# Three pads that move the weights' tiles against the moving operands of the matmuls

## The chip, the cores and the metric

One core of a Trainium2 chip runs the whole program once. The metric is the device time of one execution in microseconds (us). The engines are named as in the profile: PE is TensorE's matmul, PEld its weight load, DVE is VectorE, ACT ScalarE, POOL GpSimd, SP the queue that issues most DMAs. SBUF addresses below are bytes within a partition, and all of them follow from the order and the sizes in which the program allocates its tiles.

## The reference

Two blocks of two layers each over 256 tokens of width 2048, all in float32:

```
for l in range(2):                       # first block
    h = rms_norm(x, norm_w[l]);  p = h @ w_in[l]          # 2048 x 6668
    y = concat(window attention, conformer convolution, gated delta rule)   # all from p
    x = x + y @ w_out[l]                                   # 2048 x 2048
for l in range(2):                       # second block
    h = rmsnorm(x, ln1_g[l]);  proj = h @ w_in[l]          # 2048 x 6176
    x = x + concat(differential attention, GLA, retention) @ w_o[l]
    h = rmsnorm(x, ln2_g[l])
    u = conv3(h @ w_up[l]);  a, g = split(u)               # 2048 x 11264
    x = x + (a * silu(g)) @ w_down[l]                      # 5632 x 2048
return rmsnorm(x, final_g)
```

## The kernel before

All large products are made by one helper, `proj_t_unit` (lines 356 to 386). The residual x lies transposed in SBUF: features in the partitions, the 256 tokens along the row, four tiles of 512 features. Float32 precision is had by splitting both factors into a rounded part and a remainder (`split`, lines 249 and 250, and `norm_h`, lines 287 and 290): the normed residual becomes the tiles `hh` and `hl`, the weights become `wh` and `wl`. For each block of 128 x 128 weights, `product` issues three matmuls of 256 columns: wh with hh (L372), wh with hl (L373), wl with hh (L374). The weights are the stationary operand, loaded by PEld for each matmul (512 bytes of each partition), and the activations are the moving one (1024 bytes of each partition).

`wunit` brings the weights in units of 512 x 512: a DMA into `wr`, then ACT rounds into `wh` and DVE subtracts into `wl`, each with four buffers of 4096 bytes. The order of the instructions on each engine is made by the tile scheduler from the order of the program and its priorities.

Stages in order of time: `block1` twice (projections, attention, convolution, delta rule, then `add_x` with w_out), then `block2`, `ffn`, `block2`, `ffn`. In the blocks the matmuls of attention and delta rule are mixed into the stream by `pump`. In `ffn` the stream has nothing but `proj_t_unit`: eleven blocks of 512 columns of a and of g with the moving operand `hh`/`hl`, in two groups (six and five), and after each group the down projection with the activations `ah`/`al` as the moving operand. In a layer that is 1408 products with the normed residual and 704 with the activations, of three matmuls each.

What moves in `add_x` of the blocks are the tiles `yh`/`yl` (`put_y`). In `block1` the units 0 and 1 lie in the pool `hp`, where `hh` and `hl` also live, unit 2 has the tag "b4" and unit 3 the tag "z4". In `block2` the units 0 and 2 lie in `hp`, units 1 and 3 have the tag "p4".

**Addresses.** The pools are allocated one behind the other: `cp` (constants, with a first tile "pad0"), `hp` from 20160, `wp` behind it, `sp`, then the pool of the stage. Every buffer of `hh`, `hl`, `wr`, `wh`, `wl` is 4096 bytes, so all buffers of `hp` lie at 192 modulo 512, and all of `wh` and `wl` at 256 modulo 512, since "pad1" at the head of `wp` takes 64 bytes. The rows of a tile that one matmul or load reads start at multiples of 512 bytes in it. So one number, the start of the weights less the start of the moving operand modulo 512, tells how the two reads stand to each other; it is called the offset here. By the allocation it is, in the kernel before: 64 for `hh`/`hl`, for `yh`/`yl` in `hp`, and for `ah`/`al` in both FFN layers; 448 for `yh`/`yl` of tag "b4"; 160 for tag "z4"; 192 for tag "p4". In `proj_unit` (the untransposed projections, L424 to L426) the roles are changed: slices of `hh`/`hl` are stationary and 512 columns of the weights move.

Of the kernel before, what the change touches and what calls it, by code (L numbers as in the profile page):

```python
# [10 lines left out]
F32 = mybir.dt.float32  # L11
# [8 lines left out]
P = 128  # L20
# [113 lines left out]
class _Kernel:  # L134
    def __init__(self, ctx, tc, A):
        self.ctx, self.tc, self.nc, self.A = ctx, tc, tc.nc, A
        self.bg, self.ph, self.final = [], None, False
        self.cp = ctx.enter_context(tc.tile_pool(name="cp", bufs=1))
        self.cp.tile([P, 8], F32, name="pad0")
        self.hp = ctx.enter_context(tc.tile_pool(name="hp", bufs=4))  # L140
        self.wp = ctx.enter_context(tc.tile_pool(name="wp", bufs=3))
        self.wp.tile([P, 16], F32, name="pad1", bufs=1)
        self.sp = ctx.enter_context(tc.tile_pool(name="sp", bufs=2))
        self.pm = ctx.enter_context(tc.tile_pool(name="pm", bufs=2, space=PSUM))
        self.ps = ctx.enter_context(tc.tile_pool(name="ps", bufs=4, space=PSUM))
        self.dp = ctx.enter_context(tc.tile_pool(name="dp", bufs=1, space=DRAM))
        nc = self.nc
        self.base = self.cp.tile([P, 3 * P], F32, name="base")
        self.ident, self.le, self.gt = (self.base[:, i * P:(i + 1) * P] for i in range(3))
        self.ones = self.cp.tile([P, P], F32, name="ones")  # L150
        nc.vector.memset(self.ones, 1.0)
        self.lmask = self.cp.tile([P, 7, P], mybir.dt.uint8, name="lmask")
        self.xd = [A["xt"][g] for g in range(4)]
        self.gws = self.cp.tile([P, 112], F32, name="gws")
        self.fg = self.gws[:, 96:112]
        self.early = None
# [858 lines left out]
    def attention(self):  # L1015
# [9 lines left out]
        for t in range(2):  # L1025
            yield
            nc.vector.tensor_mul(qk[t], qk[t], r[:, t].unsqueeze(2).broadcast_to([P, 16, 64]))
            for i, (h0, h1) in enumerate(((0, 12), (12, 16))):
                n = h1 - h0
                xr = qk[t][:, h0:h1, 0:16]  # L1030
                a = self.sml([P, 12, 16], "ra", 2)
                b = self.sml([P, 12, 16], "rb", 2)
                bro = lambda v: v.unsqueeze(1).broadcast_to([P, n, v.shape[-1]])
                nc.vector.tensor_mul(a[:, :n], xr, bro(tb[:, t, i, 0]))
                nc.vector.tensor_mul(b[:, :n, 0:8], xr[:, :, 8:16], bro(tb[:, t, i, 1, 0:8]))
                nc.vector.tensor_mul(b[:, :n, 8:16], xr[:, :, 0:8], bro(tb[:, t, i, 1, 8:16]))
                nc.vector.tensor_add(xr, a[:, :n], b[:, :n])
            nc.gpsimd.tensor_copy(kd[t], qk[t][:, 12:16].unsqueeze(2).broadcast_to([P, 4, 2, 64]))
# [414 lines left out]

    def ffn(self, l, follow):
        nc, A = self.nc, self.A
        fc = self.param(A["fc2"][l], "fc2")
        cw = [fc[:, 2 * NF * i:2 * NF * (i + 1)] for i in range(3)]
        cb = fc[:, 6 * NF:]
        for b0, b1 in ((0, 6), (6, 11)):
            act = []  # L1460
            for b in range(b0, b1):
                cv = []
                for s in range(2):
                    ps = self.proj_t(A["w_up_2"][l], [(s * FF + b * 512, 512)])
                    u = self.tt("u", [P, 4, T], "u")
                    with self.tc.high_priority():
                        nc.vector.tensor_mul(u, ps, self.bcn(4))
                    c = self.ph.tile([P, 4, T], F32, tag=f"c{s}", name=f"c{s}", bufs=2)
                    col = lambda t, q: t[:, s * NF + b * 4 + q:s * NF + b * 4 + q + 1]
                    for q in range(4):  # L1470
                        nc.scalar.activation(c[:, q], u[:, q], AF.Identity, bias=col(cb, q), scale=col(cw[1], q))
                    for q in range(4):
                        nc.vector.scalar_tensor_tensor(c[:, q, 1:], u[:, q, :T - 1], col(cw[0], q), c[:, q, 1:],
                                                       op0=ALU.mult, op1=ALU.add)
                    for q in range(4):
                        nc.vector.scalar_tensor_tensor(c[:, q, :T - 1], u[:, q, 1:], col(cw[2], q), c[:, q, :T - 1],
                                                       op0=ALU.mult, op1=ALU.add)
                    cv.append(c)
                nc.scalar.activation(cv[1], cv[1], AF.Silu)
                nc.vector.tensor_mul(cv[0], cv[0], cv[1])  # L1480
                ah = self.ph.tile([P, 4, T], F32R, tag="ah", name="ah", bufs=7)
                al = self.ph.tile([P, 4, T], F32R, tag="al", name="al", bufs=7)
                self.split(cv[0], ah, al)
                act.append((ah, al, b * 512))
            self.add_x(A["w_down_2"][l], act, follow=follow if b1 == 11 else None)
# [121 lines left out]
```

## Time and profile before

| | |
|---|---|
| three runs | 3399.01, 3340.39 and 3395.86 us, median 3395.86 us |
| the profiled execution | 3369.48 us, of which the span from the first to the last instruction is 3367.7 us |
| PE busy | 3308.9 us (98%), 26498 matmuls |
| DVE, ACT, POOL busy | 2175.3 us (65%), 1636.5 us (49%), 259.8 us (8%) |
| mean granted TensorE clock | 0.988 |
| DMA | 602.64 MB, 179 GB/s over the span |

The busy time of PE is the union of matmuls that overlap (a matmul's record is about 280 ns long while the next one starts some 115 ns after it), so a busy share near 100% says that PE never waits, not how fast it goes. How fast it goes is read from the starts: the time from one matmul's start to the next, by the timeline or by the number of matmuls in a window.

### The profile page before, as it was taken

How to read it: one execution, taken by the hardware profiler on the slowest of the kernel's cores; microseconds unless marked ns; L12 is line 12 of the kernel's file. 1: busy time of each engine (PE TensorE's matmuls, PEld its weight loads, DVE VectorE, ACT ScalarE, POOL GpSimd, SP SyncE). 2: the span in 40 equal slices, each digit the busy share in tenths (PEclk: the TensorE clock that was granted, in tenths of full speed). 3: DMA queues.
4: the chain of work that ended last, by engine and by line, in shares of the span. 5: the costliest groups of instructions: out<-in, count | busy, mean ns of one | idle time of the engine just before them, and what ended most of it. 6: DMA issues, size and time to landing. Idle time of an engine off the chain costs nothing. (4 is left out here: it accounts for less than half of the span.)

```text
span 3367.7 us, 63948 instructions
## 1 busy us (share of the span) xinstructions
PE 3308.9 (98%) x26498; PEld 3191.5 (95%) x26498; DVE 2175.3 (65%) x3183; ACT 1636.5 (49%) x2202; POOL 259.8 (8%) x477
## 2 busy tenths in 40 slices
PE   8999989999999999999999999999999999999998
PEld 8899989899998988999999999999899999999998
DVE  8887558886565557666654776555665666546664
ACT  5555444554455444455543554554454455435453
POOL 1210010210010010100000000200101000000000
PEclk9999989999999999999999999999999999999999
DMA  7554476553566555566656665655545555555554
GB/s 221 153 166 135 163 205 191 150 172 112 177 218 208 160 163 154 187 190 198 195 193 194 193 194 195 212 155 159 171 148 188 189 186 185 188 188 185 187 186 144
DMA packets 351652, 602.64 MB, mean 179 GB/s; under 512 B 35314, under 2 KB 92154, under 8 KB 351360
## 3 DMA queue, kind: packets, MB, share of 16 engines
q1 hardware_dynamic: 346800, 585.15, 55.7%
q0 software_dynamic: 4560, 13.40, 1.4%
q8 instruction: 207, 3.39, 0.4%
q14 instruction: 85, 0.70, 0.1%
HBM read 589.40 MB, written 11.15 MB: 178 GB/s over the span
## 5 line engine op out<-in xcount | busy, mean ns | idle before, releaser
L250 DVE TENSOR_TENSOR wl<-wr,wh 128x1024 fp32r<-128x1024 f32 (+2 forms) x1094 | 1308.0, 1198 | 880.7 <-ACT wh L249 878.0
L249 ACT ACTIVATE wh<-wr 128x1024 fp32r<-128x1024 f32 (+2 forms) x1096 | 1128.8, 1032 | 1436.0 <-PE pt L373 1131.4
L372 PE MATMUL pt<-hh,wh 128*128 128x256 f32 x5184 | 1457.8, 281 | 8.3 <-ACT wh L249 8.3
L374 PE MATMUL pt<-hh,wl 128*128 128x256 f32 x5184 | 1457.8, 281 | 3.6 <-DVE wl L250 3.6
L373 PE MATMUL pt<-hl,wh 128*128 128x256 f32 x5184 | 1453.0, 280 | 0.0
L372 PEld LDWEIGHTS pt<-hh,wh 128*128 128x128 f32 x5184 | 985.3, 190 | 21.2 <-ACT wh L249 9.6
L374 PEld LDWEIGHTS pt<-hh,wl 128*128 128x128 f32 x5184 | 979.4, 189 | 9.0 <-DVE wl L250 4.4
L373 PEld LDWEIGHTS pt<-hl,wh 128*128 128x128 f32 x5184 | 980.8, 189 | 4.5 <-issue 4.1
L372 PE MATMUL pt<-ah,wh 128*128 128x256 f32 x1328 | 369.6, 278 | 0.0
L373 PE MATMUL pt<-al,wh 128*128 128x256 f32 x1328 | 369.6, 278 | 0.0
L374 PE MATMUL pt<-ah,wl 128*128 128x256 f32 x1328 | 369.6, 278 | 0.0
L372 PE MATMUL pt<-yh,wh 128*128 128x256 f32 x1024 | 292.4, 286 | 12.4 <-ACT wh L249 7.7
L373 PE MATMUL pt<-yl,wh 128*128 128x256 f32 x1024 | 292.3, 285 | 2.0 <-DVE yl L250 2.0
L374 PE MATMUL pt<-yh,wl 128*128 128x256 f32 x1024 | 291.3, 285 | 1.2 <-DVE wl L250 1.2
L372 PEld LDWEIGHTS pt<-ah,wh 128*128 128x128 f32 x1328 | 251.9, 190 | 0.0
L373 PEld LDWEIGHTS pt<-al,wh 128*128 128x128 f32 x1328 | 249.2, 188 | 0.0
L374 PEld LDWEIGHTS pt<-ah,wl 128*128 128x128 f32 x1328 | 249.2, 188 | 0.0
L372 PEld LDWEIGHTS pt<-yh,wh 128*128 128x128 f32 x1024 | 198.3, 194 | 13.6 <-ACT wh L249 8.4
L373 PEld LDWEIGHTS pt<-yl,wh 128*128 128x128 f32 x1024 | 198.3, 194 | 3.3 <-DVE yl L250 3.3
L374 PEld LDWEIGHTS pt<-yh,wl 128*128 128x128 f32 x1024 | 199.0, 194 | 1.7 <-DVE wl L250 1.7
L425 PE MATMUL pn<-wl,hh 128*128 128x512 f32 (+1 forms) x448 | 170.1, 380 | 0.8 <-DVE wl L250 0.7
L426 PE MATMUL pn<-wh,hl 128*128 128x512 f32 (+1 forms) x448 | 169.4, 378 | 0.0
(585 smaller groups left out, 3091.5 us busy)
## 6 DMA issues: line engine op xcount, KB each, us to landing
wr<-in_w_up_dram SPq DMA_DIRECT2D x352, 512.0 KB, 4.0
wr<-in_w_in_dram SPq DMA_DIRECT2D x320, 512.0 KB, 3.7
wr<-in_w_down_dram SPq DMA_DIRECT2D x176, 512.0 KB, 4.7
wr<-in_w_in_dram SPq DMA_DIRECT2D x158, 256.0 KB, 3.0
wr<-in_w_out_dram SPq DMA_DIRECT2D x64, 512.0 KB, 4.1
wr<-in_w_o_dram SPq DMA_DIRECT2D x64, 512.0 KB, 4.1
xs<-x SPq DMA_DIRECT2D x8, 512.0 KB, 3.8
x<-xs SPq DMA_DIRECT2D x8, 512.0 KB, 8.1
```

Source lines behind the costliest of these rows:

```text
L249: self.nc.scalar.activation(hi, src, AF.Copy)
L250: self.nc.vector.tensor_sub(lo, src, hi.bitcast(F32))
L372: nc.tensor.matmul(o, h[:, kk, cs], hi[:, k], start=start, stop=False, skip_group_check=True)
L373: nc.tensor.matmul(o, h[:, kk, cs], lo[:, k], start=False, stop=False, skip_group_check=True)
L374: nc.tensor.matmul(o, l[:, kk, cs], hi[:, k], start=False, stop=last and k == 3, skip_group_check=True)
L425: nc.tensor.matmul(o, xh[:, k, ts], l[:, kk, :n], start=False, stop=False)
L426: nc.tensor.matmul(o, xl[:, k, ts], h[:, kk, :n], start=False, stop=last and k == 3)
```

## The change

It makes "pad1" 256 bytes longer, so that `wp` and all that is allocated behind it lies 256 bytes further up, and adds a tile "pad2" as the first tile of each FFN layer's pool, 320 bytes in layer 0 and 448 bytes in layer 1, so that `ah` and `al` (and the other tiles of the FFN's pool) move up by that much more. To make room, the small tiles `ra` and `rb` of the rotary step in `attention` have one buffer instead of two. No tile of a pad is written or read.

```
@@ -139,7 +139,7 @@
         self.cp.tile([P, 8], F32, name="pad0")
         self.hp = ctx.enter_context(tc.tile_pool(name="hp", bufs=4))
         self.wp = ctx.enter_context(tc.tile_pool(name="wp", bufs=3))
-        self.wp.tile([P, 16], F32, name="pad1", bufs=1)
+        self.wp.tile([P, 80], F32, name="pad1", bufs=1)
         self.sp = ctx.enter_context(tc.tile_pool(name="sp", bufs=2))
@@ -1028,8 +1028,8 @@
                 xr = qk[t][:, h0:h1, 0:16]
-                a = self.sml([P, 12, 16], "ra", 2)
-                b = self.sml([P, 12, 16], "rb", 2)
+                a = self.sml([P, 12, 16], "ra")
+                b = self.sml([P, 12, 16], "rb")
                 bro = lambda v: v.unsqueeze(1).broadcast_to([P, n, v.shape[-1]])
@@ -1453,6 +1453,7 @@
     def ffn(self, l, follow):
         nc, A = self.nc, self.A
+        self.sml([P, (80, 112)[l]], "pad2")
         fc = self.param(A["fc2"][l], "fc2")
```

By the allocation the offsets become: 320 for `hh`/`hl` and for `yh`/`yl` in `hp`; 256 for `ah`/`al` in layer 0 and 128 in layer 1. The tags "b4", "z4" and "p4" lie behind `wp` and move with it (by 256 bytes, or 1280 bytes down where they stand behind `ra` and `rb`, which is the same modulo 512), so 448, 160 and 192 stay. In `proj_unit` the stationary slices of `hh` lie at 192 instead of 448 from the moving weights.

## Rows read from the trace of the kernel before

**Rows 1.** The page: span, and busy time of each engine.
```profile
span 3367.7 us, 63948 instructions
PE 3308.9 (98%) x26498; PEld 3191.5 (95%) x26498; DVE 2175.3 (65%) x3183; ACT 1636.5 (49%) x2202; POOL 259.8 (8%) x477
```

**Rows 2.** The page, 40 slices: the granted TensorE clock in tenths.
```profile
PEclk9999989999999999999999999999999999999999
```

**Rows 3.** Groups of instructions, whole span: count, busy us, mean ns, idle before.
```profile
L374 PE MATMUL pt<-hh,wl 128*128 128x256 f32 x5184 | 1457.8, 281 | 3.6 <-DVE wl L250 3.6
L372 PE MATMUL pt<-hh,wh 128*128 128x256 f32 x5184 | 1457.8, 281 | 8.3 <-ACT wh L249 8.3
L373 PE MATMUL pt<-hl,wh 128*128 128x256 f32 x5184 | 1453.0, 280 | 0.0
...
L424 PE MATMUL pn<-wh,hh 128*128 128x512 f32 (+1 forms) x448 | 169.4, 380 | 0.0
```

**Rows 4.** Waits of PE, whole span: total us, times, longest.
```profile
PE pt L372 <- ACT wh L249: 16.0, 6, 5.6
```

**Rows 5.** Windows, the two FFN layers: length, busy (count), clock, DMA share, GB/s.
```profile
1459.30:2170.00 710.70, 710.70 (x6273) 710.61 (x6273) 453.05 (x506) 354.38 (x392) 16.19 (x15) 1.00 0.61 193
...
2624.40:3353.00 728.60, 728.60 (x6188) 728.54 (x6186) 441.08 (x489) 346.55 (x387) 9.29 (x8) 1.00 0.58 183
```

**Rows 6.** Windows of 30 us, PE: up and down projection, layers 0 and 1.
```profile
1500.00:1530.00 30.00, 30.00 (x268) 1.00 0.63 197
1750.00:1780.00 30.00, 30.00 (x268) 1.00 0.60 193
2700.00:2730.00 30.00, 30.00 (x257) 1.00 0.57 180
2920.00:2950.00 30.00, 30.00 (x257) 1.00 0.58 183
```

**Rows 7.** Groups of instructions, 1500:2140 (layer 0), then 2660:3300 (layer 1).
```profile
L373 PE MATMUL pt<-hl,wh 128*128 128x256 f32 x1239 | 342.0, 276 | 0.0
...
L373 PE MATMUL pt<-hl,wh 128*128 128x256 f32 x1258 | 353.5, 281 | 0.0
```

**Rows 8.** Timeline of PE, w_out of block1, layer 1: first matmul of each unit.
```profile
946.53 0.28 PE L372 MATMUL pt<-yh,wh 128*128 128x256 f32 x1
...
952.29 0.28 PE L372 MATMUL pt<-yh,wh 128*128 128x256 f32 x1
...
957.74 0.28 PE L372 MATMUL pt<-yh,wh 128*128 128x256 f32 x1
...
963.18 0.28 PE L372 MATMUL pt<-yh,wh 128*128 128x256 f32 x1
...
968.83 0.28 PE L372 MATMUL pt<-yh,wh 128*128 128x256 f32 x1
...
974.59 0.28 PE L372 MATMUL pt<-yh,wh 128*128 128x256 f32 x1
```

**Rows 9.** Timeline of PE, w_o of block2: layer 0 (1413 on), layer 1 (2555 on).
```profile
1413.21 0.28 PE L372 MATMUL pt<-yh,wh 128*128 128x256 f32 x1
...
1418.87 0.28 PE L372 MATMUL pt<-yh,wh 128*128 128x256 f32 x1
...
1424.31 0.28 PE L372 MATMUL pt<-yh,wh 128*128 128x256 f32 x1
...
2555.26 0.28 PE L372 MATMUL pt<-yh,wh 128*128 128x256 f32 x1
...
2560.91 0.28 PE L372 MATMUL pt<-yh,wh 128*128 128x256 f32 x1
...
2566.57 0.28 PE L372 MATMUL pt<-yh,wh 128*128 128x256 f32 x1
```

**Rows 10.** The rotary step's instructions: min/median/max ns, first and last start.
```profile
L1034 DVE TENSOR_TENSOR ra<-qk,atb x8: 213/281/352, 133.6 to 638.2; 128x192 f32<-128x192 f32 x4, 128x64 f32<-128x64 f32 x4
L1037 DVE TENSOR_TENSOR qk<-ra,rb x8: 210/278/346, 137.6 to 640.2; 128x192 f32<-128x192 f32 x4, 128x64 f32<-128x64 f32 x4
```

More of the change, by code (lines that the diff above doesn't have):

```diff
@@ L141, in __init__ @@
         self.wp = ctx.enter_context(tc.tile_pool(name="wp", bufs=3))
-        self.wp.tile([P, 16], F32, name="pad1", bufs=1)
+        self.wp.tile([P, 80], F32, name="pad1", bufs=1)
         self.sp = ctx.enter_context(tc.tile_pool(name="sp", bufs=2))
@@ L1030, in attention @@
                 xr = qk[t][:, h0:h1, 0:16]
-                a = self.sml([P, 12, 16], "ra", 2)
-                b = self.sml([P, 12, 16], "rb", 2)
+                a = self.sml([P, 12, 16], "ra")
+                b = self.sml([P, 12, 16], "rb")
                 bro = lambda v: v.unsqueeze(1).broadcast_to([P, n, v.shape[-1]])
@@ L1455, in ffn @@
         nc, A = self.nc, self.A
+        self.sml([P, (80, 112)[l]], "pad2")
         fc = self.param(A["fc2"][l], "fc2")
```

## The prediction

> **What bounds the kernel now.** I read the page first. PE is busy for 3308.9 of the 3367.7 us and DVE for 65% [rows 1], the granted clock is at its upper level, 2.4 GHz, in all but a short stretch [rows 2], and the longest sum of waits of PE on another engine is 16.0 us in six waits [rows 4]. So PE bounds the kernel, and a change that adds or removes no matmul can matter only through the time from one matmul's start to the next. The costliest groups are the three matmuls of `product`, 5184 each with the normed residual [rows 3]. What is to be seen next is that this time is not one number. In the two FFN layers PE is busy in every microsecond at a clock of 1.00, with the same instructions: layer 0 has 6273 matmuls in 710.70 us, 113.3 ns each, and layer 1 has 6188 in 728.60 us, 117.7 ns each [rows 5]. Windows of 30 us hold 268 matmuls in layer 0 and 257 in layer 1, in the up projection and in the down projection alike [rows 6], and the matmul's own record is 276 ns in the one and 281 ns in the other [rows 7]. By the allocation the addresses in the two layers are the same. So at offset 64 there are two levels, 113.3 and 117.8 ns, and a stream that runs without a break stays at the level at which it set out.
>
> The timeline gives the other offsets, 48 matmuls a unit, first start to first start, in one unbroken stream. In w_out of `block1` [rows 8]: offset 160 takes 952.29 - 946.53 = 5.76 us, 120.0 ns each; offset 64 takes 5.45 and 5.44 us, 113.5 and 113.3 ns; offset 448 takes 968.83 - 963.18 = 5.65 us, 117.7 ns; offset 160 again 5.76 us. In w_o of `block2` [rows 9]: offset 192 takes 1418.87 - 1413.21 = 5.66 us, 117.9 ns, and offset 64 behind it 5.44 us, 113.3 ns; in the other layer 192 takes 5.65 us and 64 behind it 5.66 us, both 117.8 ns. So the level goes with the offset within one stream and within 10 us, with no wait between: 64 has 113.3 or 117.8, 192 and 448 have 117.8, 160 has 120.0, and a stream that passes 192 comes back to the level that it had before.
>
> The two levels also account for the spread of the times. One FFN layer at 117.7 instead of 113.3 costs 6188 x 4.45 ns = 27.5 us. The profiled execution has one layer of each kind and 3369.5 us; with both at 113.3 it would have 3342.0, with both at 117.7 it would have 3369.5 + 6273 x 4.45 ns = 3397.4. The three runs are 3340.4, 3395.9 and 3399.0. So the median run, 3395.9, is read as two layers at the upper level. This also says what can be told: the same kernel's times differ by 1.8%, and about 2% is what a measurement of it can tell from no change.
>
> **The change part by part.** The pads themselves issue nothing: they are tiles that are never written or read, no instruction, no DMA, no wait. Their cost is room, paid by `ra` and `rb`. There the second use of a buffer has to come behind the addition that reads the first (L1037), on the same in-order engine; the eight additions have a median of 278 ns and the eight multiplications 281 ns [rows 10]. If DVE stood still for all of them it would be 8 x 0.56 = 4.5 us of DVE; DVE idles for a third of the span [rows 1] and PE in that stretch runs on projections, so I take nothing, and 4.5 us as the upper bound. Behind these instructions DVE's queue has `wl` subtractions of the unit after next, for which four buffers stand ready.
>
> The offset of `hh`/`hl` goes from 64 to 320. This concerns 2816 x 3 = 8448 matmuls in the FFN layers (1408 products a layer), (5184 - 2816) x 3 = 7104 in the blocks [rows 3], and those of `yh`/`yl` that lie in `hp`. The trace shows no stretch at 320. The bounds from the rows are the least and the most that any offset shows, 113.3 and 120.0 ns. The offset of `ah`/`al` goes from 64 to 256 in layer 0 and to 128 in layer 1, 704 x 3 = 2112 matmuls each, with the same bounds, because 256 and 128 do not occur either. For all three I take 113.3: it is the floor of every stream in the trace, it is the level at which the nearest measured offset, 64, also runs, and the two offsets that only show 117.8 are left alone by the change. That choice is the weak step of this forecast. The untransposed projections (448 groups of three, L424 to L426 [rows 3]) change their own offset from 448 to 192; no row separates the levels there, and by the half-way gap of 4.5 ns on 1344 matmuls it is 6 us either way, taken as nothing.
>
> The sum, against the profiled execution: layer 0 stays at 113.3, nothing; layer 1 goes down by 27.5 us; the blocks, where both levels occur in an unknown share, have 7104 x 4.45 = 31.6 us between all at the lower and all at the upper level, so half way is 16 us of gain or loss, taken as nothing. 3369.5 - 27.5 = 3342.0 us. Against the median run this is -1.6%. What comes next when PE goes faster: DVE is busy for 453.05 us and ACT for 354.38 us of layer 0's 710.70 [rows 5], where PE already runs at 113.3 without a wait, so nothing else becomes the bound.
>
> **The rivals.** First, a two-level stream as before. 192 and 448 differ by 256 and have the same level; if the pattern repeats every 256 bytes, 320 is 64 again, and each layer is thrown to one of two levels by how its stream happens to start. Then the times stay 3342, 3369 or 3397, the middle one the most even guess. The Trainium skill speaks for the same outcome by another road: "TensorE: Matmul & The Clock Gate", section "Step-by-step: what each phase is for", has PE read the weights and the moving operand through two independent ports, so that loading takes nothing from the running matmul; by it no offset should matter and the change does nothing. The trace does not agree, with 120.0, 113.3 and 117.7 ns in one stream. As a mechanism of this kernel it remains possible that the tile and not its offset makes those levels, which again gives 3369.
>
> Second, on the other side: the new offsets have only the upper level, as 192 and 448 do. Then layer 0 loses 6273 x 4.45 = 27.9 us and the blocks up to 16: 3369.5 + 27.9 + 16 = 3413 us, above the median of before. The point from which it decides is a mean of 117.8 ns in both layers; two of the four measured offsets are of this kind. If instead the new offsets are as bad as 160, at 120.0 ns, layer 0 loses 6273 x 6.7 = 42 us, layer 1 6188 x 2.3 = 14 us, and the blocks 7104 x (120.0 - 115.5) = 32 us: 3457 us.
>
> Third, a level under 113.3. No row has one. The same page of the skill, section "Back-to-back issue gap", gives N/2.4 + 2.5 ns between matmuls of N columns, an estimate of 109.2 ns for 256 columns; by it the sum would fall by another 4.1 ns on some 23,000 matmuls, 94 us. The trace does not show it in any stream, though PE never waits there.
>
> **How the numbers follow.** The lower level in both layers: 0.42, 3342 us, and 3326 to 3342 if the blocks gain as well. Two levels as before: 0.27, 3342 to 3400. Only the upper level: 0.22, 3397 to 3425. As 160: 0.05, about 3457. A level under 113.3: 0.04, below 3320. The forecast is the likeliest, 3342. The range goes from 3318 to 3414, which leaves out the two rare cases and the upper part of the slow one. Faster by over 2% means below 3328: the rare case under 113.3, the lower third of the first case and a little of the measurement's own spread, 0.2. Slower by over 2% means above 3464, the upper end of the 160 case: 0.04. The rest, 0.76, is within 2%.
>
> **What the profile of the changed kernel would show.** If the forecast is right, windows of 30 us in both layers hold 268 matmuls, in the up and in the down projection, with records of 276 ns. If the first rival is right, one layer or both have 257 with 281 ns, and repeated runs differ by some 27 us. If only the down projection is at 257, the fault lies in 256 or 128 alone, 2112 x 4.45 = 9.4 us a layer. If the second rival is right, no stretch of L372 to L374 with `hh` comes under 117.7. The units of w_out and w_o with 448, 160 and 192 should stand at 117.8, 120.0 and 117.8 as before; if they don't, it is not the offset that makes the level. The forecast would also be wrong if the scheduler, given one buffer for `ra` and `rb`, orders PE's stream anew so that PE waits for more than the 16.0 us.

## The result, and the profile after

The change made no difference that can be told from the medians: 3385.91 us over 22 runs (3370.17 to 3396.67) against 3396.14 us over 22 runs of the kernel before on the same chip (3340.39 to 3403.93). The forecast was 3342. The ratio given with its interval is 1.0072 [1.005, 1.0095]; it leaves out every run that is over 1.5% above the fastest of its kernel, and of before these are the 13 runs near 3399, so it compares the change with before's faster executions only. The medians of all runs stand as 3385.91 / 3396.14 = 0.997, and their means are 3385.4 and 3385.9 us.

What did change is the spread. The 22 runs of before lie in three groups: one at 3340.4, eight from 3366.8 to 3375.6, thirteen from 3393.3 to 3403.9. These are the 3342, 3369 and 3397 of the prediction, which lie 27 to 28 us apart. The runs of the change lie without such steps within 26.5 us. The groups at both ends are gone.

The profiled execution of the change took 3386.81 us, before's 3369.48. The page of the change, span, busy time and granted clock by slices, as in [rows 1, 2]:

```profile
span 3385.0 us, 63948 instructions
PE 3320.9 (98%) x26498; PEld 3202.8 (95%) x26498; DVE 2175.6 (64%) x3183; ACT 1634.4 (48%) x2202; POOL 257.8 (8%) x477
...
PEclk9999999999999999999999999999999999999999
```

The same 26498 matmuls keep PE busy for 12 us more, at the same clock, so it is again the pace of the stream. All that PE stands idle, the span less its busy time, is 64.1 us for 58.8, and its largest sum of waits is 17.2 us for 16.0 [rows 4], though the longest of them is 8.2 for 5.6 (total, times, longest):

```profile
PE pt L372 <- ACT wh L249: 17.2, 5, 8.2
```

Windows of 30 us of the change, PE: length, busy (count), clock, DMA share, GB/s. The first four lie in layer 0 (first up group, first down projection, second up group, second down projection), the last four in layer 1, in the same order; [rows 6] are their counterparts:

```profile
1500.00:1530.00 30.00, 30.00 (x258) 1.00 0.62 194
1750.00:1780.00 30.00, 30.00 (x252) 1.00 0.58 186
1900.00:1930.00 30.00, 30.00 (x267) 1.00 0.65 202
2100.00:2130.00 30.00, 30.00 (x253) 1.00 0.58 187
2700.00:2730.00 30.00, 30.00 (x257) 1.00 0.57 178
2950.00:2980.00 30.00, 30.00 (x255) 1.00 0.57 185
3100.00:3130.00 30.00, 30.00 (x267) 1.00 0.63 195
3300.00:3330.00 30.00, 30.00 (x255) 1.00 0.58 186
```

Before, a layer had one count throughout, 268 or 257. Now each layer has three: 257 or 258 in the first up group, 252 to 255 in the down projections, 267 in the second up group. The timeline gives the exact paces: the first matmul of each of these stretches of the change (start in us, record length in us), four in layer 0 and four in layer 1:

```profile
1457.32 0.28 PE L372 MATMUL pt<-hh,wh 128*128 128x256 f32 x1
...
1711.01 0.28 PE L372 MATMUL pt<-ah,wh 128*128 128x256 f32 x1
...
1849.24 0.29 PE L372 MATMUL pt<-hh,wh 128*128 128x256 f32 x1
...
2066.86 0.28 PE L372 MATMUL pt<-ah,wh 128*128 128x256 f32 x1
...
2647.54 0.28 PE L372 MATMUL pt<-hh,wh 128*128 128x256 f32 x1
...
2901.23 0.28 PE L372 MATMUL pt<-ah,wh 128*128 128x256 f32 x1
...
3037.94 0.28 PE L372 MATMUL pt<-hh,wh 128*128 128x256 f32 x1
...
3255.53 0.28 PE L372 MATMUL pt<-ah,wh 128*128 128x256 f32 x1
```

The first up group has 2154 matmuls in the unbroken stream: 1711.01 - 1457.32 = 253.69 us, 117.8 ns each, at offset 320. The down projection behind it has 1152 in 138.23 us: 120.0 ns each, at offset 256. The second up group has 1920 in 217.62 us: 113.3 ns, again at 320. In layer 1 the same three are 117.8, 118.7 (136.71 us, offset 128) and 113.3 (217.59 us). The last down projection of each layer, 960 and 959 matmuls, runs at the pace of the first, 120.0 and 118.7.

With these paces the difference closes. Layer 0 takes 253.7 + 138.2 + 217.6 + 960 x 0.120 = 724.7 us for 6186 matmuls that at before's 113.3 took 701.1: 23.6 us lost, of which 9.6 are the first up group's, at the upper level here and at the lower in the profile of before, by the chance of the two executions. Layer 1 takes 253.7 + 136.7 + 217.6 + 959 x 0.1187 = 721.8 us for 6185 that at 117.78 took 728.5: 6.7 us won. 3369.5 + 23.6 - 6.7 = 3386.4, measured 3386.81.

The units of w_out in `block1` of layer 1, which answer to [rows 8] (timeline, first matmul of each unit, offsets 320, 320, 448, 160):

```profile
949.55 0.28 PE L372 MATMUL pt<-yh,wh 128*128 128x256 f32 x1
...
955.02 0.28 PE L372 MATMUL pt<-yh,wh 128*128 128x256 f32 x1
...
960.46 0.28 PE L372 MATMUL pt<-yh,wh 128*128 128x256 f32 x1
...
966.10 0.28 PE L372 MATMUL pt<-yh,wh 128*128 128x256 f32 x1
...
971.85 0.28 PE L372 MATMUL pt<-yh,wh 128*128 128x256 f32 x1
```

5.47 and 5.44 us at 320 (5.45 and 5.44 at 64 before), 5.64 at 448 (5.65), 5.75 at 160 (5.76). Offsets that the change left alone kept their pace, and 320 does what 64 did.

### The profile page after: what moved, and what is told of

Same layout as the page of the kernel before. It is cut to its first block, busy times and chain, and to the rows that moved or that the text cites. A ratio compares the mean times of both kernels' runs of the same rounds, so it can differ in the third digit from the quotient of the medians.

```text
span 3385.0 us, 63948 instructions
## 1 busy us (share of the span) xinstructions
PE 3320.9 (98%) x26498; PEld 3202.8 (95%) x26498; DVE 2175.6 (64%) x3183; ACT 1634.4 (48%) x2202; POOL 257.8 (8%) x477
## 5 line engine op out<-in xcount | busy, mean ns | idle before, releaser
L424 PE MATMUL pn<-wh,hh 128*128 128x512 f32 (+1 forms) x448 | 169.4, 380 | 0.0
```

The source lines that it names most:

```text
L424: nc.tensor.matmul(o, xh[:, k, ts], h[:, kk, :n], start=first and k == 0, stop=False)
```

## The experiments

The theory drawn from the two traces is Theory A: the pace goes with the offset modulo 256. 320 is 64 again, with two levels; 256 costs 120.0 ns and 128 costs 118.7; and a stretch at one of the two throws the stream to one level, which the next stretch at 64 keeps. The rivals stand with each run. Before ran beside each kernel, on the same chip; its medians there were 3378.53 (25 runs, beside e1 to e4), 3379.01 (13, beside e5 to e8) and 3380.81 (25, beside e9 to e11). None of the pads alters the order of PE's matmuls: in the traces of e2, e3, e7 and e8 all 26498 matmuls of PE stand in the order of before, and in those of e4, e5 and e6 too, but that 96 of them read the other tile. The single `ra` and `rb` do alter the order, as the last runs show.

### One part alone: the longer pad1 (e1_pad1_only)

```
+        self.wp.tile([P, 80], F32, name="pad1", bufs=1)
...
+                a = self.sml([P, 12, 16], "ra")
+                b = self.sml([P, 12, 16], "rb")
```

> The change without its FFN pads: normed residual at offset 320, activations back at 64. Theory A (the level depends on the offset modulo 256, and the two FFN pads are what cost): as the kernel before, each FFN layer one unbroken stream at 113.3 or at 117.8 ns a matmul, up and down projection alike, times near 3342, 3370 or 3398 us, never between 3375 and 3390 by more than the blocks' few us; a window of 30 us in the down projection holds 268 or 257 matmuls. Theory B (offset 320 itself is worse than 64, or the single buffer of ra and rb costs): the down projection may be at 113.3 or 117.8, but the times keep the change's mean near 3386, with the loss in the up projection or in the blocks.

Measured: 3388.6 us median of 10 (3356.56, then six from 3382 to 3390.6, then three from 3411.6 to 3420.7), ratio 0.9975 [0.9929, 1.0022]. The three steps of before are back, some 30 us apart, and the profiled execution, 3384.47 us, has one layer of each kind. Windows of it, PE, first up group of layer 0 and of layer 1:

```profile
1500.00:1530.00 30.00, 30.00 (x267) 1.00 0.67 192
...
2700.00:2730.00 30.00, 30.00 (x258) 1.00 0.65 187
```

So 320 is 64 in the FFN layers. But each of the three groups lies some 12 us above before's (3345.5, 3370 to 3381 and 3402.6 to 3410.3 on the same chip). That belongs to the blocks, and is taken up by the last three runs.

### One part alone: pad2 (e2_pad2_only)

```
     def ffn(self, l, follow):
+        self.sml([P, (80, 112)[l]], "pad2")
```

> The kernel before with the two FFN pads alone: normed residual at 64, activations at 256 (layer 0) and 128 (layer 1), ra and rb with two buffers. Theory A: the down projections run at 120.0 ns in layer 0 and 118.7 ns in layer 1, the second group of the up projection in each layer at 113.3 ns whatever the first was, and the first at 113.3 or 117.8; times 3342 + 14.1 + 11.3 = 3367 plus 0, 9.6 or 19.2 us, so 3367 to 3387, like the change itself. Theory B: the times and levels of the kernel before, near 3342, 3370 or 3398 us, with only the down projection differing.

Measured: 3382.02 us median of 10 (3375.73 to 3395.51), ratio 1.0034 [1.0009, 1.0059]. The profiled execution, 3395.51 us, behaves as the change does. Windows of it, PE: first down and second up group of layer 0, then the second up group of layer 1:

```profile
1750.00:1780.00 30.00, 30.00 (x253) 1.00 0.59 180
1900.00:1930.00 30.00, 30.00 (x267) 1.00 0.64 185
...
3100.00:3130.00 30.00, 30.00 (x268) 1.00 0.69 197
```

The down projection at 120.0 ns and the lower level behind it come from pad2 alone, with `hh` at 64. The change's effect on the FFN layers is that of pad2.

### The activations at 0 and 384 (e3_act_0_384)

```
+        self.sml([P, (16, 48)[l]], "pad2")
```

> The kernel before with FFN pads of 64 and 192 bytes: activations at offset 0 in layer 0 and 384 in layer 1, normed residual at 64. Theory A (period 256): the down projection of layer 0 at 120.0 ns as at 256, of layer 1 at 118.7 ns as at 128, and the second group of the up projection at 113.3 ns in both layers. Rival (period 512): other levels than at 256 and 128, anything from 113.3 to 120 ns.

Measured: 3385.61 us, one run. Windows of it, PE: first down of layer 0 (offset 0), second up group behind it, first down of layer 1 (offset 384):

```profile
1750.00:1780.00 30.00, 30.00 (x253) 1.00 0.62 185
1900.00:1930.00 30.00, 30.00 (x267) 1.00 0.67 196
...
2950.00:2980.00 30.00, 30.00 (x255) 1.00 0.59 188
```

0 has the count of 256, and 384 that of 128. The pattern repeats every 256 bytes, and the change's 256 is the place where both reads start together.

### A short stretch to set the level: another weights' tile at 256 (e4_reset)

If a stretch at another offset sets the level, a short one would do. In the second product of each FFN layer, one unit (48 matmuls) gets its weights in tiles `wha`, `wla` of the FFN's pool, at offset 256 from `hh`; all else stays at 64.

```
-                h = self.wp.tile([P, 2, 512], F32R, tag="wh", name="wh", bufs=4)
...
+                if self.alt:
+                    h = self.ph.tile([P, 2, 512], F32R, tag="wha", name="wha", bufs=2)
...
+                    if turn:
+                        self.sml([P, 64], "pad3")
+                    ps = self.proj_t(A["w_up_2"][l], [(s * FF + b * 512, 512)], alt=turn)
+                    if turn:
+                        self.sml([P, 64], "pad4")
```

> The kernel before with one unit of weights of each FFN layer (the fifth of the first group, 48 matmuls) in buffers of its own at offset 256 from the normed residual; everything else at 64. Theory A (a stretch at 256 leaves the stream at the lower level): 48 matmuls at about 120 ns, and all that follows in the layer at 113.3 ns, in both layers, in every execution: 3342 us plus 2 x 48 x 6.7 ns = 0.6 us, and up to 2 x 1 us where the first four units ran at 117.8; 3335 to 3352 us, without the steps of 27 us. Rival (the change's lower level after the down projection was chance, or needs the long stretch): layers at 113.3 or 117.8 as before, times near 3342, 3370 or 3398 us.

Measured: 3407.44 us median (3403 to 3412.5), ratio 1.0064 [1.0035, 1.0093]. The expectation missed. Timeline of the profiled execution, layer 0, PE: a matmul in the unit ahead, the first of the 48, the first behind them, the 17th product behind that:

```profile
1470.68 0.28 PE L377 MATMUL pt<-hh,wh 128*128 128x256 f32 x1
...
1475.45 0.28 PE L377 MATMUL pt<-hh,wha 128*128 128x256 f32 x1
...
1481.20 0.28 PE L377 MATMUL pt<-hh,wh 128*128 128x256 f32 x1
...
1486.86 0.28 PE L377 MATMUL pt<-hh,wh 128*128 128x256 f32 x1
```

1475.45 - 1470.68 = 4.77 us for 14 products, 113.6 ns a matmul; 5.75 us for the 48 with `wha`, 119.8; and 5.66 us for the 48 behind them, 117.9. The stream came in at the lower level and left at the upper, and stayed there: both layers ran at 117.8 to the end, and all runs lie within 10 us, where before's third group lies on that chip (3402.6 to 3410.3). A stretch of 6 us does set the level of 700 us, but this one sets the wrong one.

### The same from the other side (e5_moving_reset, the best version)

Here the weights stay and the moving operand is elsewhere: ACT copies `hh0`, `hl0` into `ch`, `cl` at offset 256, and the same 48 matmuls use them. The products are the same, four copies of about 1.05 us on ACT are added, two a layer.

```
+                    xs = None
+                    if (b, s) == (0, 1):
+                        self.sml([P, 80], "pad3")
+                        ch = self.ph.tile([P, 4, T], F32R, tag="ch", name="ch", bufs=1)
+                        cl = self.ph.tile([P, 4, T], F32R, tag="cl", name="cl", bufs=1)
+                        nc.scalar.activation(ch, self.hi[0].bitcast(F32), AF.Copy)
+                        nc.scalar.activation(cl, self.lo[0].bitcast(F32), AF.Copy)
+                        self.sml([P, 48], "pad4")
+                        xs = ([ch] + self.hi[1:], [cl] + self.lo[1:])
+                    ps = self.proj_t(A["w_up_2"][l], [(s * FF + b * 512, 512)], xs)
```

> The kernel before with a copy of the first unit of the normed residual (both parts) at offset 256, used for 48 matmuls early in each FFN layer; everything else at 64. Theory A' (what sets the level is the jump of the moving operand from offset 256 back to 64, as behind the down projections; the weights' jump in the earlier kernel left 117.8): 48 matmuls at 120.0 ns and the rest of both layers at 113.3 ns in every execution, near 3342 us plus the blocks' spread, 3335 to 3355. Rival (48 matmuls don't do it, or it needs the 960 or 1152 of a down projection): the rest of the layers at 117.8 ns in every execution, 3398 to 3412 us, or either level by chance, in steps of 27 us.

Measured: 3345.63 us median (3339.92 to 3352.59), ratio 0.9924 [0.9891, 0.9956]; against the median of all runs of before, 3345.63 / 3379.01 = 0.990. Timeline of the profiled execution (3341.97 us), layer 0, PE: a matmul of the unit ahead, the first of the 48, the first behind them, the 17th product:

```profile
1455.77 0.28 PE L372 MATMUL pt<-hh,wh 128*128 128x256 f32 x1
...
1460.72 0.28 PE L372 MATMUL pt<-ch,wh 128*128 128x256 f32 x1
...
1466.47 0.29 PE L372 MATMUL pt<-hh,wh 128*128 128x256 f32 x1
...
1471.93 0.28 PE L372 MATMUL pt<-hh,wh 128*128 128x256 f32 x1
```

117.9 ns ahead (4.95 us for 14 products), 119.8 in the 48, 113.7 behind them, with the first steps of the new level in it. Windows of layer 0 and of layer 1, first up group:

```profile
1500.00:1530.00 30.00, 30.00 (x267) 1.00 0.68 195
...
2700.00:2730.00 30.00, 30.00 (x267) 1.00 0.69 195
```

Both layers are at the lower level, the 3342 that the prediction gave to this state. This kernel beats both others, before by about 1%: its slowest run, 3352.59, lies under all of before's but one, 3338.6. A copy that moves at offset 64 was not tried, but before itself goes from `hh` to `ah` and back at 64, and its level stays [rows 6], so a mere change of tile does not set the level.

### The weights' side at 128 (e6_reset_128)

The edit is shown against e4.

```
-                        self.sml([P, 64], "pad3")
+                        self.sml([P, 32], "pad3")
...
-                        self.sml([P, 64], "pad4")
+                        self.sml([P, 96], "pad4")
```

> As the kernel with one unit of weights in buffers of their own, but at offset 128 instead of 256. Theory A' (a jump of the weights leaves the stream at 117.8, whatever the offset): 48 matmuls at about 118.7 ns, then 117.8 ns in both layers, near 3400 us. Rival (it is the offset that is left that decides: 256 leaves the upper level after 48 matmuls, 128 the lower): 113.3 ns behind it in both layers, near 3342 us.

Measured: 3351.12 us, one run. In layer 0 the stream came in at 113.3, in layer 1 at 117.8; behind the 48 matmuls both layers ran at 113.3. Windows of it, PE, first up groups:

```profile
1500.00:1530.00 30.00, 30.00 (x267) 1.00 0.69 202
...
2700.00:2730.00 30.00, 30.00 (x268) 1.00 0.67 192
```

So a stretch with other weights can leave the lower level; it is not the side alone but the side with the offset (256 from the weights' side leaves 117.8, 256 from the moving side and 128 from the weights' side leave 113.3).

### The rest of the map (e7_act_96_32, e8_act_224_160)

```
+        self.sml([P, (120, 8)[l]], "pad2")      # e7: activations at 96 and 32
...
+        self.sml([P, (88, 104)[l]], "pad2")     # e8: activations at 224 and 160
```

> The kernel before with the activations at offset 96 in layer 0 and 32 in layer 1, both between offsets whose levels are known modulo 256 (0: 120.0, 64: 113.3 or 117.8, 128: 118.7). Theory (the level changes step by step with the offset): values between the neighbours, 115 to 120 ns, none under 113.3. Rival (some offset off the multiples of 64 has one level only, the lower): 113.3 ns or less in one of the down projections.

> The kernel before with the activations at offset 224 in layer 0 and 160 in layer 1. Theory: 160 gives 120.0 ns, as the tag z4 of the blocks shows, and 224, between 192 (117.8) and 256 (120.0), something from 117.8 to 120 ns; behind 160 the next group of the up projection runs at 113.3 ns, as the units behind z4 do. Rival: 224 at 113.3 ns.

Measured: 3368.01 and 3386.45 us, one run each. Windows of the kernel with 96 and 32, layer 0, PE: first up group (64), down at 96, second up group (64):

```profile
1500.00:1530.00 30.00, 30.00 (x267) 1.00 0.68 195
1750.00:1780.00 30.00, 30.00 (x258) 1.00 0.61 192
1900.00:1930.00 30.00, 30.00 (x257) 1.00 0.65 191
```

Windows of the kernel with 224 and 160: down at 224 in layer 0, down at 160 in layer 1, second up group behind that:

```profile
1750.00:1780.00 30.00, 30.00 (x260) 1.00 0.62 185
...
2950.00:2980.00 30.00, 30.00 (x252) 1.00 0.56 179
3100.00:3130.00 30.00, 30.00 (x257) 1.00 0.64 186
```

96 takes the stream from the lower level to the upper; behind 160 it stays at the upper, which that layer had ahead of it too (257 in the window 2700:2730), where 113.3 was expected. By the timeline the paces are, modulo 256: 0: 120.0; 32: 118.3; 64: 113.3 or 117.8; 96: 117.3 or 118.7, by the level it is entered from; 128: 118.7; 160: 120.0; 192: 117.8; 224: 116.7 ns. Of these only 64 has 113.3, and nothing is under it.

### The blocks: the single buffers, and 320 there (e9_reset_ra_rb, e10_reset_pad1, e11_reset_again)

With the moving-side reset the FFN layers stand at one level, so a few us in the blocks can be read from medians. The three ran on the same chip: the reset with single `ra` and `rb`; this with the longer pad1 as well; and the reset as it was.

```
-                a = self.sml([P, 12, 16], "ra", 2)
-                b = self.sml([P, 12, 16], "rb", 2)
+                a = self.sml([P, 12, 16], "ra")            # e9 and e10
+                b = self.sml([P, 12, 16], "rb")
...
-        self.wp.tile([P, 16], F32, name="pad1", bufs=1)
+        self.wp.tile([P, 80], F32, name="pad1", bufs=1)    # e10 alone
```

> The kernel of the moving-side reset (offset 64 everywhere, 48 matmuls a layer against a copy of the normed residual at offset 256), and in it `ra` and `rb` with one buffer, the change's third part alone. With the reset both FFN layers stand at 113.3 ns in every execution, so the 27 us steps are gone and a cost in the blocks can be read. Theory A (the single buffers change the order of TensorE's stream in block1, and this is where the kernel with the first pad alone lost its 12 us against the kernel before): some 12 us over the same kernel with two buffers, with the FFN layers the same in length. Rival B (it was the 320 in the blocks): the same time as with two buffers, within 3 us. Rival C (the forecast's bound, DVE standing still for 4.5 us): up to 4.5 us more, in block1 alone.

> The same with the longer pad1 as well: `hh` and `hl` at 320, the activations at 64, single `ra` and `rb`, and the moving-side reset. Theory A: the same time as the kernel of the reset with single `ra` and `rb`, within 3 us, because 320 is 64 modulo 256 and the pad costs nothing. Rival B: the 12 us come here and not there. Both expect 113.3 ns behind the 48 matmuls of each FFN layer; if 320 answers to the reset in another way, a layer stands at 117.8, 27 us more.

> The kernel of the moving-side reset unchanged, as the base for the two beside it on the same chip: 3340 to 3353 us as before, its ratio to the kernel before within the earlier interval; both FFN layers at 113.3 ns behind the 48 matmuls. If the level behind the reset is not set by the program, single executions some 27 us longer would occur.

Measured, ten runs each: 3358.7 us (3354.24 to 3363.57) with the single buffers, 3358.78 (3353.93 to 3361.23) with the longer pad1 as well, 3349.72 (3343.09 to 3355.21) with neither; ratios to before 0.9954 [0.9918, 0.9989], 0.9968 [0.9923, 1.0012] and 0.9953 [0.992, 0.9985]. The ratios, which hang on what the executions of before happened to be, do not tell the three apart; the runs themselves do, since nine of the ten with neither lie under the fastest of the other twenty. Behind the 48 matmuls all six FFN layers were at 113.3, whichever level they came in with. The single buffers cost 9.0 us, and 320 in place of 64, with all that moves by 256 in the blocks, costs 0.1, which is nothing.

Waits of PE (total, times, longest), the sum of fourteen windows of 100 us from 0 to 1400, in which PE's busy time is the first number, and the eight additions L1037 as in [rows 10], of the kernel with the single buffers and then of the one without. First with:

```profile
PE pt L372 <- ACT wh L249: 21.0, 5, 12.9
```

```profile
sum 1400.00, PE 1344.15 PEld 1263.61 DVE 951.37 ACT 676.56 POOL 173.84; mean PE 96.01 PEld 90.26 DVE 67.95 ACT 48.33 POOL 12.42
```

```profile
L1037 DVE TENSOR_TENSOR qk<-ra,rb x8: 208/282/355, 138.8 to 661.2; 128x192 f32<-128x192 f32 x4, 128x64 f32<-128x64 f32 x4
```

Then without:

```profile
PE pt L372 <- ACT wh L249: 15.9, 6, 6.8
```

```profile
sum 1400.00, PE 1354.03 PEld 1274.24 DVE 959.02 ACT 683.71 POOL 180.45; mean PE 96.72 PEld 91.02 DVE 68.50 ACT 48.84 POOL 12.89
```

```profile
L1037 DVE TENSOR_TENSOR qk<-ra,rb x8: 207/278/345, 138.6 to 642.8; 128x192 f32<-128x192 f32 x4, 128x64 f32<-128x64 f32 x4
```

Until 1400 us, which is before the first FFN layer, PE is busy for 9.9 us less, and the longest wait for weights has gone from 6.8 to 12.9 us. The traces tell how. With two buffers the additions run in pairs, in the first layer at 138.6 and 138.8 and at 142.6 and 142.9 us. With one buffer each addition has to come ahead of the next multiplications, with other work of DVE between them, and the four are at 138.8, 142.1, 150.1 and 153.9. So the last addition comes 11.0 us later in the first layer and 18.4 us later in the second. PE's stream is ordered anew between 141 and 914 us, which is in `block1`: 3742 of the 26498 matmuls stand at another place, among them those of the delta rule (L724, L765), which come earlier, between those of `product`. At the 7000th matmul, behind that stretch, the kernel with the single buffers is 8.7 us late. How much of it is the late additions and how much the order was not taken apart. With 320 and with 64 the order is the same, and so is the time; the kernel of the change and e1 have this order too.

## Why the prediction was wrong

**What bounds the kernel** was right. PE's pace is the time; no other engine became late in the FFN layers, the clock of every window shown is 1.00, and the two changed sums close to 0.4 us on paces alone.

**Two levels at offset 64, 27 us a layer** was right. Before's runs group, each time, as the prediction worked it out from one layer of each kind, and with both layers set to the lower level the profiled time was 3341.97, where the prediction gave 3342.0 to that state. That the two agree so closely is luck, since the ten runs of that kernel lie from 3339.92 to 3352.59. What the prediction took as given by how the stream starts can be set by the program, with 48 matmuls.

**The step that failed** is "For all three I take 113.3". For `hh` at 320 the first rival was right: the pattern repeats every 256 bytes (e1, e3 and e10 show it), so 320 changed nothing. For `ah` and `al` even the first rival was too good: 256 has 120.0 ns and 128 has 118.7, so the second rival's worst case, "as bad as 160", is what came true of 256, though only for the 2112 matmuls of a layer that use it. The term -27.5 us for layer 1 came out as -6.7 in the profiled execution, and the term 0 for layer 0 as +23.6. There was a row that could have warned: of the four offsets measured before, only 64 had ever shown 113.3, and [rows 8] had 160 at 120.0. The choice of the floor rested on 64 being the nearest offset measured. It is the nearest to none of the three: modulo 512, as the prediction counts, 320 lies 128 from 192 and from 448 but 256 from 64, 256 lies 64 from 192, and 128 lies 32 from 160; modulo 256, 128 still lies nearer to 160, and 256 as near to 192 as to 64.

**What the prediction did not have** is that a stretch at 256 or 128 decides the level of what follows. It gave back part of the loss: the second up group, 1920 matmuls a layer, ran at 113.3 in every profile in which the activations stood there. That is why the steps of 27 us are gone: what is left open in each layer is the first up group, 2154 x 4.45 ns = 9.6 us. The prediction held the level fixed within an unbroken stream, which is true only at one offset or past 192, 448 and 160 [rows 8, 9]. In its own sum, with the right sizes: 3342.0 + 2112 x 6.67 ns + 2112 x 5.33 ns = 3367.4 with both first groups at the lower level, and 3386.6 with both at the upper; the profiled execution has the second, 3386.81. But nine of the 22 runs lie above 3390, which these paces do not reach; with the 9.0 us of the single buffers the sum gives 3376.4, 3386.0 and 3395.6 for none, one and both of the first groups at the upper level, and the median is 3385.91. So it is partly luck that the one profiled execution meets the sum without them.

**The single `ra` and `rb`**, "I take nothing, and 4.5 us as the upper bound", was too small: 9.0 us between medians. The bound counted DVE standing still for the eight pairs of instructions; what the buffer held up was the last addition, by 11.0 and 18.4 us, with DVE at other work meanwhile. With it came what the prediction named last, a new order of PE's stream with a longer wait. The single profile of the change has that order, but its time does not show the cost: its layer 0 stream begins at 1457.32, before's at 1459.26. One execution is too coarse for this: two profiled executions of the reset kernel, with the same paces in the FFN layers, have spans of 3340.2 and 3351.6 us, on two chips.

**The untransposed projections**, taken as nothing with 6 us either way, were nothing: their offset changes between e9 and e10, and the medians differ by 0.1 us. With a period of 256 that had to be so, since 448 and 192 are then the same offset.

**The other rivals.** A level under 113.3 appeared nowhere on the map. The Trainium skill, "TensorE: Matmul & The Clock Gate", section "Step-by-step: what each phase is for", has the weight load take no SBUF read bandwidth from the running matmul. The offset experiments do not agree that the two are independent: the same matmuls in the same order take 113.3 to 120.0 ns by nothing but the addresses of the two operands and the level that the stream is at. Whether it is bandwidth that one takes from the other, no run shows. The Trainium skill, "TensorE: Matmul & The Clock Gate", section "Back-to-back issue gap", gives the formula behind the third rival's 109.2 ns for an isolated matmul, and says that a stream with a weight load for each matmul is paced by both. The prediction left that out, so 109.2 ns was no measure for this stream, and no run here shows an isolated gap.

**How a layer comes by its level** can be followed further back than the start of its stream. Windows of before, PE: the 83 matmuls with `hh` that come ahead of the norm's small matmuls, the 66 that come between those, and the long stream of layer 0:

```profile
1442.00:1449.00 7.00, 7.00 (x64) 1.00 0.50 151
1451.20:1458.20 7.00, 7.00 (x61) 1.00 0.72 239
1459.60:1466.60 7.00, 7.00 (x64) 1.00 0.63 199
```

By the starts these are 113.3, 117.8 and 113.3 ns. Between the first two lie the four small matmuls that write `xss` (L325), between the last two the four that write `bcps` (L231). Each of the two interruptions turned the level over in all 26 FFN layers of the thirteen profiles, ten times from 113.3 to 117.8 and back, sixteen times the other way round. So a layer starts at the level of the 83 matmuls ahead of the norm, and before has it already in w_o, 113.3 at offset 64 ahead of layer 0 and 117.8 ahead of layer 1 [rows 9]. The first rival's words, that a layer is thrown to a level by how its stream happens to start, put the choice too late.

**What stays open** is why w_o comes to the one level in one execution and to the other in the next, and what decides the level that a stretch leaves behind. 256 leaves 113.3 when the moving operand is displaced and 117.8 when the weights are; 128 leaves 113.3 on either side; 96 turned 113.3 into 117.8. 160 left the stream as it had come, at 117.8 behind the activations and at 113.3 in [rows 8], where the units at 64 have 113.3. That it is the two operands' reads colliding in SBUF is a reading that fits a period of 256 bytes; no run shows it.

## What to carry to other kernels

When a busy engine's pace differs between two stretches of the same instructions, read it by the starts, sort the stretches by the addresses of the operands, and move one operand at a time: the offset of the weights from the moving operand was worth up to 6% of a matmul here, and the best one (64 modulo 256) was already in use. Do not give an unmeasured offset the floor; take the mean of those measured. Where the same program runs at two levels, look for a short stretch that sets the level: here it was worth 33 us between the medians, while no other offset came under the 113.3 ns of 64. And before costing a lost buffer at the time of its own instructions, see what else will come between them, and whether the scheduler will order the other engines' streams anew.

## What the runs showed of the hardware

Matmuls of 256 columns in float32 with a weight load each have a start-to-start time of 113.3 to 120.0 ns at a granted clock of 1.00, set by the offset of the two operands modulo 256 bytes and, at 64 and 96, by the level that the stream is at. At 64 there are two stable levels, 113.3 and 117.8 ns. A stream of over 700 us without a break stays at one of them, and 48 matmuls at another offset can move it to the other: it went from 117.8 to 113.3 behind 48 matmuls at 256 with a displaced moving operand, and from 113.3 to 117.8 behind 48 at 256 with displaced weights. Four small matmuls (of 1 or of 128 columns) within the stream turned it over, both ways, in every one of the 26 FFN layers profiled. Three matmuls, one product, take 340.0, 353.3 or 360.0 ns at the three commonest paces.
